# A hybrid transformer block on one core: modulation vectors as column-grouped TensorE products, and the convolution norm moved behind its last taps

## The chip, the cores and the metric

The kernel runs on one core of a Trainium2 chip. The metric is the device time of one execution in microseconds. Three runs of the kernel before gave 1427.99, 1431.49 and 1431.73 us, a median of 1431.49. The engines are named as in the profile: PE is TensorE (PEld its weight loads), DVE is VectorE, ACT is ScalarE, POOL is GpSimd, and SP is the engine that issues every DMA of this kernel. Each engine works through its own queue in a fixed order.

## The reference

One block of a network over 512 tokens of width 1024, with 256 context tokens, all in 32-bit floats:

```
mod_x = split((silu(c) @ w_ada + b_ada), 6)          # six vectors of 1024; the same of c_ctx for the context
h  = rmsnorm(x, g_norm1) * (1 + mod_x[1]) + mod_x[0] # hc the same of ctx with mod_c
u_rw, u_cv, u_ml, u_gate = split(h @ w_in)           # the RWKV and mLSTM parts also of hc
ya = rwkv mixer (8 heads, both directions)           # a state recurrence over context and tokens
yc = mlstm mixer (4 heads, both directions)
yb = silu(layernorm(depthwise_conv(a * sigmoid(g)), cv_lnw, cv_lnb))   # 31 taps, 512 channels
x  = x + mod_x[2] * ((ga*(ya@p_a) + gb*(yb@p_b) + gc*(yc@p_c)) @ w_out) # ga, gb, gc = sigmoid(u_gate)
h  = rmsnorm(x, g_norm2) * (1 + mod_x[4]) + mod_x[3]
x  = x + mod_x[5] * (square(relu(h @ w_mlp1)) @ w_mlp2)
out = rmsnorm(x, g_final)
```

So vectors 0 and 1 are needed at once, and 2 to 5 only after the three branches.

## The kernel before, in words

Large matrix products are split: each operand is a rounded part (hi) and a rest (lo), and a product is three products, hi by hi, hi by lo and lo by hi. A half block of weights (128x512) is loaded by SP into a ring of three raw buffers (tag "raw", L149), ACT makes hi (L152) and POOL makes lo (L153). `dense` (L262) multiplies one block of 128 output columns with all tokens in 24 products. Small products in plain 32-bit floats stand in the trace as two instructions each.

The stages, in the order in which they are emitted:

- Prologue (L170 to L231). The tokens are normalized, the first two modulation vectors are made, and the modulated tokens are laid down transposed. The weights `wada` for vectors 0 and 1 are 8 loads of 1 MB into six buffers. For each of four groups of 512 columns, 8 products (L215) with a stationary operand of two columns (the silu of `c` and of `c_ctx`) are summed in two rows of PSUM, copied (L217), transposed in four pieces (L220) and applied.
- Convolution and operand stage (L276 to L473). Channel tiles 0 and 1 of the convolution are gated and go through their 31 taps on DVE (L291). Then, for each of four pairs of RWKV heads, `operands` (L338 to L394) makes what the recurrence reads, twice per pair: loads BK and rd from other tiles (L348 to L353), small products `plora` (L358), exponentials on ACT, two scans on DVE, products on POOL (L379 to L386) and DVE (L389, L393), and stores to DRAM. `values` (L434 to L442) follows for all pairs.
- mLSTM stage (L477 to L514): `front` and `back` of each of four heads. The taps of channel tiles 2 and 3 (L495) are emitted after `back(0)`; then the pool `CZ` that they use closes (L498), and the RWKV pool `rwa` opens in memory on the same side. Its first loads (L946) and the Gram products and inverses of the first pair (`ctx(0)`, `lat(0)`) are emitted there, before the heads that are left. Six gate blocks follow.
- RWKV stage (L517 to L690). For each of four pairs a chain of 12 steps with three phases each (L1113, L1119, L1128: a product on PE, an eviction on ACT, the new state on DVE at L1129). `weave` spreads over it the preparation of the next pair, the last pair's output, and products of `dense_`: the 18 other gate blocks (L531), then the projections of the convolution and the mLSTM (L610). In the last pair (j = 3) it also spreads `conv_norm` (L552 to L593), which loads the four convolution tiles, normalizes over channels and activates them, and `modulations` (L630 to L653), which makes vectors 2, 3 and 4: for each of six groups of 512 columns, 8 loads (L623) and 8 accumulations on DVE (L625, L627), then small products that sum over the partitions (L640, L651).
- Merge and MLP (`merge`, L1239 on). What is left of the modulations is emitted first (`for _ in mods: pass`), then the projection of the RWKV branch (L701), the output projection (L1281), the second norm, and the MLP (L1350, L1281). The last vector is made in the same way inside the MLP's loop by `last_modulation`, after blocks 8 and 16, and read from DRAM at the end.

A planner fixes the order of each engine's queue ahead of the run, from estimated durations and with the order of emission as the priority (`schedule_with_timeline_sim=True`); the steps of the RWKV chain get a raise (`BOOST`), and what `weave` spreads is held behind the chain's last instruction on its engine (`paced`).

Of the kernel before, what the change touches and what calls it, by code (L numbers as in the profile page):

```python
# [7 lines left out]
F32 = mybir.dt.float32  # L8
# [52 lines left out]
def rsqrt(nc, S, x, n, name="rsq"):  # L61
    """1 / sqrt of the few columns x (overwritten): a first guess from the exponent, three Newton steps."""
# [14 lines left out]
def build(tc, wblk, wada, xin, cin, params, lora, consts, rowp, out, dbg=None):  # L77
# [42 lines left out]
    sc = K.tile([P, KT, 2], F32, name="sc")  # L120
# [13 lines left out]
    sp["m5", 0] = DR.tile([1, D], F32, name="sp_m5")  # L134
# [28 lines left out]
    # ------------------------------------------------------------------ norm, first modulation, hT  # L163
# [20 lines left out]
    V.tensor_tensor(sc.rearrange("p k c -> p (k c)"), tc_[:, :], C("cc", 0, 16), ALU.mult)  # L184
# [59 lines left out]
    # ------------------------------------------------------------------ input projections  # L244
# [23 lines left out]
    # ------------------------------------------------------------------ convolution branch  # L268
# [69 lines left out]
    def operands(j, h, kb, r):  # L338
        """What the products of head h of pair j read, for both directions, one on each half of the partitions."""
# [6 lines left out]
        # rows of the products with U and with V, in this order in the first half, swapped in the second  # L346
# [48 lines left out]

    t = shifted(12, True, "vj", 2)
# [5 lines left out]
    # keys and the normalized keys of every pair  # L402
# [42 lines left out]
    for j in range(4):  # L445
# [30 lines left out]
    # convolution and mLSTM branches  # L476
# [10 lines left out]
    eg.close()  # L487
    st = [None] * 4
    tiles = [(i, CZ.tile([P, 752], F32, name=f"cz{i}")[:, :], CZ.tile([P, NT], F32, name=f"cy{i}")[:, :]) for i in (2, 3)]
# [6 lines left out]
    for i, z, y in tiles:  # L496
        SY.dma_start(sp["yb", i][:, :], y)
# [1004 lines left out]
```

## Time and profile before

| what | value |
|---|---|
| median of three runs | 1431.49 us (1427.99 to 1431.73) |
| profiled execution: span from its first to its last instruction | 1429.6 us (the profile gives no other time for it) |
| granted TensorE clock, mean | 0.934 |
| PE, DVE, POOL, ACT busy | 1271.3, 903.0, 689.4, 496.4 us |
| bytes moved | 187.81 MB, mean 131 GB/s |
| 64 loads of 256 KB for vectors 2 to 5 (wad) | median 3.8 us from issue to landing |
| 296 loads of weight halves (raw) | median 2.8 us from issue to landing |
| DVE accumulations of vectors 2 to 5 (L627) | 56 instructions, 56.7 us |

Times are microseconds of one execution, from the span's start. Busy time is an average over stages with different limits, so the stages have to be read one by one. A PE instruction's duration in the profile is modelled and overlaps with the next one's; what one costs in a row of many is the distance between starts.

### The profile page before, as it was taken

The numbers are of one execution on the slowest core, as the hardware profiler recorded it, in microseconds if no ns is written. First come the engines' busy times: TensorE is split into PE (matmuls) and PEld (weight loads), VectorE is DVE, ScalarE is ACT, GpSimd is POOL, SyncE is SP. The second block draws the span as 40 slices with busy tenths as digits, with TensorE's granted clock in tenths as the row PEclk, the third lists the DMA queues.
The fourth block names the chain that finished last, engine by engine and source line by source line (L and its number), as shares of the span: only waits on it lengthen the run. The fifth ranks groups of instructions, "written<-read, shape, count | busy, mean of one in ns | idle before, by whom it ended". The sixth has DMA issues, their size and how long they took to land.

```text
span 1429.6 us, 21049 instructions
## 1 busy us (share of the span) xinstructions
PE 1271.3 (89%) x7620; PEld 985.8 (69%) x7620; DVE 903.0 (63%) x1518; ACT 496.4 (35%) x1024; POOL 689.4 (48%) x651
## 2 busy tenths in 40 slices
PE   6989986857698989789989998888999999999997
PEld 1578765635587877566757665566778888888886
DVE  2689888988736699379598895868657543300202
ACT  3422534423222222134244344532354344422322
POOL 0463499990854544233243344533455454444442
PEclk9999998887899998899699998999999999999999
DMA  9211466554162232433244134587544433343332
GB/s 363 67 60 58 119 182 205 171 182 147 39 185 72 93 107 67 128 101 100 72 135 117 45 97 156 185 258 231 205 153 146 134 111 96 111 144 99 125 96 88
DMA packets 113359, 187.81 MB, mean 131 GB/s; under 512 B 23124, under 2 KB 41812, under 8 KB 112232
## 3 DMA queue, kind: packets, MB, share of 16 engines
q1 hardware_dynamic: 113256, 186.47, 41.6%
q8 instruction: 60, 0.98, 0.3%
q14 instruction: 43, 0.35, 0.1%
HBM read 148.64 MB, written 29.40 MB: 125 GB/s over the span
## 4 chain that ended last, share of the span: by engine, by line
PE 58%; DVE 21%; DMA 7%; POOL 7%; issue 5%; ACT 2%; SPq 1%; DVEq 0%; POOLq 0%; ACTq 0%
PE pt L1281 15%; PE pd L1350 12%; PE dl L262 8%; PE dg L531 5%; POOL wlo L153 4%; PE pg L989 3%; DMA wad<-wada 3%; DVE N L1032 3%; PE pr L215 2%; DVE tmp L1030 2%; PE dc L262 2%; DVE cy L291 2%; POOL BK L386 1%; PE ch L1113 1%; DVE N L1025 1%
## 5 line engine op out<-in xcount | busy, mean ns | idle before, releaser
L153 POOL TENSOR_TENSOR wlo<-raw,whi 128x512 fp32r<-128x512 f32 x296 | 440.3, 1493 | 492.9 <-ACT whi L152 437.6
L152 ACT CAST whi<-raw 128x512 fp32r<-128x512 f32 x296 | 181.8, 618 | 358.1 <-PE pt L1281 113.8
L262 PE MATMUL dl<-hh,wlo 128*128 128x512 f32 (+1 forms) x368 | 153.6, 418 | 24.8 <-POOL wlo L153 24.7
L262 PE MATMUL dl<-hh,whi 128*128 128x512 f32 (+1 forms) x368 | 154.5, 420 | 0.7 <-DVE lf L716 0.7
L262 PE MATMUL dl<-hl,whi 128*128 128x512 f32 (+1 forms) x368 | 152.6, 415 | 0.0
L1376 DVE TENSOR_TENSOR x<-pt,modb 128x512 f32<-128x512 f32 x8 | 5.5, 689 | 154.7 <-PE pt L1281 154.7
L1350 PE MATMUL pd<-h2l,whi 128*128 128x512 f32 (+1 forms) x272 | 102.6, 379 | 0.7 <-POOL h2l L1333 0.7
L262 PEld LDWEIGHTS dl<-hh,wlo 128*128 128x128 f32 (+1 forms) x368 | 73.6, 200 | 42.1 <-POOL wlo L153 26.6
L1350 PE MATMUL pd<-h2h,wlo 128*128 128x512 f32 (+1 forms) x272 | 102.0, 377 | 0.0
L1350 PE MATMUL pd<-h2h,whi 128*128 128x512 f32 (+1 forms) x272 | 101.1, 378 | 0.2 <-ACT h2h L1330 0.2
L1281 PE MATMUL pt<-whi,h1l 128*128 128x512 f32 x256 | 99.6, 389 | 0.0
L1281 PE MATMUL pt<-whi,h1h 128*128 128x512 f32 x256 | 99.6, 389 | 0.0
L1281 PE MATMUL pt<-wlo,h1h 128*128 128x512 f32 x256 | 99.1, 389 | 0.0
L262 PEld LDWEIGHTS dl<-hh,whi 128*128 128x128 f32 (+1 forms) x368 | 73.8, 200 | 17.0 <-DVE lf L716 2.1
L262 PEld LDWEIGHTS dl<-hl,whi 128*128 128x128 f32 (+1 forms) x368 | 73.6, 200 | 15.0 <-issue 0.5
L1126 POOL TENSOR_TENSOR sps<-SV,PL 64x128 f32<-64x128 f32 x88 | 40.1, 455 | 79.0 <-DVE SV L1129 75.5
L1354 DVE TENSOR_TENSOR relu<-relu 128x512 f32<-128x512 f32 x32 | 39.5, 1238 | 56.0 <-ACT relu L1353 55.9
L627 DVE SCALAR_TENSOR_TENSOR accm<-wad,sc,accm 128x512 f32<-128x512 f32 x56 | 56.7, 1013 | 27.0 <-DMA wad<-wada 26.6
L531 PE MATMUL dg<-hh,whi 128*128 128x512 f32 x144 | 66.5, 462 | 0.0
L531 PE MATMUL dg<-hl,whi 128*128 128x512 f32 x144 | 66.4, 461 | 0.0
L531 PE MATMUL dg<-hh,wlo 128*128 128x512 f32 x144 | 65.6, 456 | 0.0
L989 PE MATMUL pg<-AL,BK 64*128 64x128 f32 (+1 forms) x384 | 59.1, 311 | 5.5 <-DVE AL L996 4.5
(388 smaller groups left out, 2942.0 us busy)
## 6 DMA issues: line engine op xcount, KB each, us to landing
raw<-wblk SPq DMA_DIRECT2D x296, 256.0 KB, 2.8
wad<-wada SPq DMA_DIRECT2D x64, 256.0 KB, 3.8
wada<-wada SPq DMA_DIRECT2D x8, 1024.0 KB, 17.5
sp_bk<-BK SPq DMA_DIRECT2D x8, 768.0 KB, 3.5
BK<-sp_bk SPq DMA_DIRECT2D x8, 768.0 KB, 4.5
sp_g<-gt SPq DMA_DIRECT2D x24, 256.0 KB, 2.1
sp_al<-al SPq DMA_DIRECT2D x8, 640.0 KB, 3.2
AL<-sp_al SPq DMA_DIRECT2D x16, 256.0 KB, 5.8
```

What stands on the lines that cost most here:

```text
L152: A.copy(hi[:, :], raw[:, :])
L153: G.tensor_tensor(lo[:, :], raw[:, :], hi[:, :], ALU.subtract)
L215: PE.matmul(pr[:, :], lhsT=sc[:, k, :], rhs=wa[q * 2 + k // 4][:, k % 4, :], start=(k == 0), stop=(k == KT - 1))
L262: PE.matmul(ps_[0:M, :], lhsT=w[:, ko:ko + M], rhs=x[seg][:, k, :], start=(n == 0), stop=(n == 3 * KT - 1))
L531: yield lambda w=w, x=x, k=k, ko=ko, n=n: PE.matmul(ps[:, :], lhsT=w[:, ko:ko + P], rhs=x[:, k, :], start=(n == 0), stop=(n == 3 * KT - 1))
L627: V.scalar_tensor_tensor(o, t[:, :], sc[:, k, 0:1], o, ALU.mult, ALU.add)
L989: PE.matmul(ps[:, i, :, :], lhsT=BK[dd, c, :, :], rhs=AL[d][dd, b0:b0 + w, :], start=True, stop=True)
L1032: V.tensor_tensor(N[:, s + 1:32, 0:s], N[:, s + 1:32, 0:s], tv, ALU.add)
L1126: last["Pool"] = G.tensor_tensor(sps[hf], SV[d][hf, c, :, :], PL[hf, c, :].unsqueeze(2).to_broadcast([64, 2, CH]), ALU.mult)
L1281: PE.matmul(pss[i][:, :], lhsT=x[:, k, ts_], rhs=w[:, :], start=(k == 0 and n == 0), stop=(k == nk - 1 and n == 2))
L1350: PE.matmul(ps[:, ts_], lhsT=w[:, ko:ko + P], rhs=x[:, k, ts_], start=(k == 0 and n == 0), stop=(k == 7 and n == 2))
L1354: V.tensor_tensor(t[:, :], t[:, :], t[:, :], ALU.mult)
```

## The change

All modulation products now use `partial`: block k of a group of 512 columns is multiplied with a stationary operand of 32 columns (the two silu columns of block k and what lies behind them) and written to the 32 PSUM partitions of column group k mod 4. Blocks 0 to 3 start a sum, blocks 4 to 7 end it. Four partial sums stand then in rows 0, 32, 64 and 96 (for `c_ctx` in the rows behind these). They are added by a product with `sel`, which has a one in those rows. In the prologue this takes the place of the sum in two rows and of the transposition. For vectors 2 to 5, `modulation(q)` is emitted in the operand stage, one group behind each call of `operands`. Its loads use the ring of raw weight buffers, its copies the buffer tagged "bo". Vectors 2 and 5 go to DRAM as rows and are read back as broadcasts; 3 and 4 are written to `b2` and `s2` at once. The DVE accumulations, `modulations` and `last_modulation` are gone, and `weave` for the last pair carries only the chain, the tail and `dense_`.

`conv_norm` is no longer a generator in the last pair. It is called behind the taps of tiles 2 and 3, on the tiles that are still there and on tiles 0 and 1 loaded again, in the pool `CZ`, and stores the four results. `projections` loads and splits them when it comes to them, and those of the mLSTM likewise only when it comes to these.

```diff
-    sc = K.tile([P, KT, 2], F32, name="sc")
+    scz = K.tile([P, 2 * KT + 30], F32, name="scz")
+    sel = K.tile([P, 2], F32, name="sel")
+    V.memset(scz[:, 2 * KT:], 0.0)
+    V.tensor_tensor(sel[:, :], ident[:, 0:2], ident[:, 32:34], ALU.add)
...
+    def partial(ps, k, w):
+        g = slice(32 * (k % 4), 32 * (k % 4) + 32)
+        PE.matmul(ps[g, :], lhsT=scz[:, 2 * k:2 * k + 32], rhs=w, start=(k < 4), stop=(k >= 4))
...
-        pr = PS0.tile([2, NT], F32, tag="pr", name="pr", bufs=2)
+        pr = PS0.tile([P, NT], F32, tag="pr", name="pr", bufs=2)
         for k in range(KT):
-            PE.matmul(pr[:, :], lhsT=sc[:, k, :], rhs=wa[q * 2 + k // 4][:, k % 4, :], start=(k == 0), stop=(k == KT - 1))
-        row = S0.tile([2, NT], F32, tag="row", name="row", bufs=2)
+            partial(pr, k, wa[q * 2 + k // 4][:, k % 4, :])
+        row = S0.tile([P, NT], F32, tag="row", name="row", bufs=2)
         A.copy(row[:, :], pr[:, :])
...
-            PE.transpose(pt[:, i, :], row[:, i * P:(i + 1) * P], ident[0:2, 0:2])
+            PE.matmul(pt[:, i, :], lhsT=row[:, i * P:(i + 1) * P], rhs=sel[:, :], start=True, stop=True)
...
+    def modulation(q):
+        ps = PSD.tile([P, NT], F32, tag="d", name="pq", bufs=ND)
+        for k in range(KT):
+            w = W0.tile([P, 512], F32, tag="raw", name="wad", bufs=NRAW)
+            SY.dma_start(w[:, :], wada[8 + q * 2 + k // 4][:, k % 4 * 512:k % 4 * 512 + 512])
+            partial(ps, k, w[:, :])
+        row = S1.tile([P, NT], F32, tag="bo", name="row")
+        A.copy(row[:, :], ps[:, :])
+        if 2 <= q < 6:
+            pc = PS1.tile([P, 4], F32, tag="n", name="pc", bufs=2)
+            for i in range(4):
+                PE.matmul(pc[:, i:i + 1], lhsT=row[:, i * P:(i + 1) * P], rhs=sel[:, 0:1], start=True, stop=True)
...
+        else:
+            m, x = q // 6, slice(q % 2 * 512, q % 2 * 512 + 512)
+            pc = PS1.tile([P, NT], F32, tag="n", name="pc", bufs=2)
+            PE.matmul(pc[0:1, :], lhsT=sel[:, 0:1], rhs=row[:, :], start=True, stop=True)
+            br = S1.tile([P, NT], F32, tag="bo", name="br")
+            SY.dma_start(br[0:1, :], rowp[m:m + 1, x])
+            V.tensor_tensor(br[0:1, :], pc[0:1, :], br[0:1, :], ALU.add)
+            SY.dma_start(sp["m", 2 + 3 * m][:, x], br[0:1, :])
...
             operands(j, h, kbs[j], rj)
+            modulation(2 * j + h)
...
+    def conv_norm(late):
+        ys = []
+        for i in range(2):
+            y = CZ.tile([P, NT], F32, name=f"cy{i}")
+            SY.dma_start(y[:, :], sp["yb", i][:, :])
+            ys.append(y[:, :])
+        ys += late
...
+        for i in range(1, 4):
+            G.tensor_tensor(total[:, :], total[:, :] if i > 1 else ys[0], ys[i], ALU.add)
...
+            V.scalar_tensor_tensor(ys[i], th, 1.0, ys[i], ALU.add, ALU.mult)
+            SY.dma_start(sp["yb", i][:, :], ys[i])
...
     taps(tiles)
-    for i, z, y in tiles:
-        SY.dma_start(sp["yb", i][:, :], y)
+    conv_norm([y for _, _, y in tiles])
     ec.close()
...
-        ys = {1: acc["yb"], 2: [operand(sp["yc", i]) for i in range(4)]}
         for b in (1, 2):
+            ys = [operand(sp[("yb", "yc")[b - 1], i]) for i in range(4)]
...
-    mods = modulations()
-    norm = conv_norm()
-    rw.weave(3, dense_, norm, mods)
+    acc["mod2b"] = acc["pool"].tile([P, D], F32, name="mod2b")
+    SY.dma_start(acc["mod2b"][:, :], sp["m", 2][:, :].partition_broadcast(P))
+    rw.weave(3, dense_)
...
-    for _ in mods:
-        pass
...
-        if fs[0] in (8, 16):
-            last_modulation(5 + fs[0] // 8, S, PS)
```

## Rows read from the trace of the kernel before

**Rows 1.** The page, the chain that ended last: shares of the span by engine.

```profile
PE 58%; DVE 21%; DMA 7%; POOL 7%; issue 5%; ACT 2%; SPq 1%; DVEq 0%; POOLq 0%; ACTq 0%
```

**Rows 2.** Stages: length, busy PE, PEld, DVE, ACT, POOL, clock, DMA share, GB/s.

```profile
180.00:322.00 142.00, 100.64 (x436) 76.32 (x434) 120.13 (x82) 55.01 (x91) 136.69 (x116) 0.86 0.62 186
...
407.00:494.00 87.00, 83.17 (x495) 71.50 (x494) 46.31 (x143) 21.39 (x40) 44.71 (x50) 0.96 0.40 119
494.00:596.00 102.00, 82.78 (x580) 68.92 (x578) 83.59 (x212) 23.45 (x44) 38.49 (x41) 0.88 0.29 94
...
863.00:942.00 79.00, 64.93 (x493) 43.73 (x492) 54.52 (x98) 37.10 (x98) 39.90 (x41) 0.91 0.58 186
942.00:1020.00 78.00, 70.00 (x326) 55.90 (x326) 61.00 (x93) 20.77 (x35) 27.66 (x19) 0.96 0.78 251
```

**Rows 3.** Timeline of the prologue: start, us, engine, line, operation, tiles, count.

```profile
13.07 6.44 PE L215 MATMUL pr<-wada,sc 128*2 128x512 f32 x8 [13.07 <-DVE rs0t L71]
...
40.78 7.03 PE L215 MATMUL pr<-wada,sc 128*2 128x512 f32 x16
...
54.79 0.79 PE L262 MATMUL dl<-hh,whi 128*128 128x512 f32 x1
```

**Rows 4.** The stage table's columns for two short stretches of the prologue.

```profile
28.00:30.00 2.00, 2.00 (x6) 0.42 (x5) 0.00 (x0) 1.15 (x2) 0.00 (x0) 1.00 1.07 422
...
34.00:36.00 2.00, 2.00 (x6) 0.43 (x5) 2.00 (x3) 1.34 (x3) 2.00 (x2) 1.00 0.41 135
```

**Rows 5.** Timeline of PE near 938 us, output products in two column halves.

```profile
938.38 0.22 PE L1095 MATMUL py<-LR,UU 128*64 128x64 f32 x1
938.43 0.22 PE L1094 MATMUL py<-AL,SV 128*64 128x64 f32 x1
938.44 0.22 PE L1095 MATMUL py<-LR,UU 128*64 128x64 f32 x1
```

**Rows 6.** Waits of SP (100 to 322 us), PE and DMA issues (180 to 322).

```profile
SPq L149 <- POOL wlo L153: 73.3, 24, 19.5
...
PE tp L434 <- DVE bo L441: 21.6, 3, 13.6
...
raw<-wblk SPq DMA_DIRECT2D x23, 256.0 KB, 4.2
```

**Rows 7.** Timelines of SP, DVE and PE: first RWKV load, last inverse, first step.

```profile
407.34 0.43 SPq L946 DMA_DIRECT2D BK<-sp_bk  x1
...
555.34 8.53 DVE L1055 STREAM_TRANSPOSE LT<-N 32x1024 f32<-32x1024 f32 x4
...
596.12 1.15 PE L1113 MATMUL ch<-SV,AL 128*64 128x64 f32 x6 [4.29 <-DMA SV<-sp_v]
```

**Rows 8.** Groups by line, 860 to 942 us: count, busy us, mean ns, idle before.

```profile
L627 DVE SCALAR_TENSOR_TENSOR accm<-wad,sc,accm 128x512 f32<-128x512 f32 x19 | 21.1, 1112 | 7.2 <-DMA wad<-wada 7.0
...
L569 DVE TENSOR_TENSOR macc<-macc,mean 128x512 f32<-128x512 f32 x4 | 3.6, 955 | 2.9 <-ACT mean L567 2.9
...
L590 DVE TENSOR_SCALAR macc<-macc,dv 128x512 f32<-128x512 f32 x4 | 2.3, 584 | 0.0
...
L573 POOL TENSOR_TENSOR ctot<-ctot,csq 128x512 f32<-128x512 f32 x3 | 4.3, 1430 | 0.9 <-ACT UV L1122 0.8
```

**Rows 9.** Timeline of PE: phases of the last pair's chain, its waits in brackets.

```profile
866.52 0.46 PE L1113 MATMUL ch<-SV,AL 128*64 128x64 f32 x8
...
867.80 0.46 PE L1119 MATMUL ch<-xc,LT 64*64 64x64 f32 x8
...
875.46 1.01 PE L1113 MATMUL ch<-SV,AL 128*64 128x64 f32 x8 [4.17 <-DVE SV L1129]
...
937.54 0.60 PE L1113 MATMUL ch<-SV,AL 128*64 128x64 f32 x5 [1.86 <-ACT UU L1132]
```

**Rows 10.** The chain of waits, a full stretch of PE; PE groups by line.

```profile
1020.45 41.72 PE pt L1281 x184
...
L663 PE MATMUL pmr<-accm,ones 128*1 128x512 f32 x4 | 2.0, 591 | 0.0
```

More of the change, by code (lines that the diff above doesn't have):

```diff
@@ L133, in build @@
         sp["z", i] = DR.tile([P, 752], F32, name=f"sp_z{i}")
-    sp["m5", 0] = DR.tile([1, D], F32, name="sp_m5")
+    for m in (2, 5):
+        sp["m", m] = DR.tile([1, D], F32, name=f"sp_m{m}")
     sp_rows = [DR.tile([4, T], F32, name=f"sp_rows{i}") for i in range(4)]
@@ L487, in build @@
     eg.close()
+    def conv_norm(late):
[5 more added lines that the diff above has]
+        ys += late
+        wide = lambda name: CZ.tile([P, 752], F32, tag="cz", name=name, bufs=2)[:, 0:NT]
+        total = CZ.tile([P, NT], F32, name="ctot")
+        for i in range(1, 4):
+            G.tensor_tensor(total[:, :], total[:, :] if i > 1 else ys[0], ys[i], ALU.add)
+        pl = PSD.tile([P, NT], F32, tag="d", name="cn", bufs=ND)
+        PE.matmul(pl[:, :], lhsT=ones[:, :], rhs=total[:, :], start=True, stop=True)
+        mean = wide("mean")
+        A.activation(mean, pl[:, :], AF.Copy, scale=1.0 / 512)
+        for i in range(4):
+            V.tensor_tensor(ys[i], ys[i], mean, ALU.subtract)
+            sq = total[:, :] if i == 0 else wide("csq")
+            A.activation(sq, ys[i], AF.Square)
+            if i:
+                G.tensor_tensor(total[:, :], total[:, :], sq, ALU.add)
+        pv = PSD.tile([P, 4], F32, tag="d", name="cv", bufs=ND)
+        for t in range(4):
+            PE.matmul(pv[:, t:t + 1], lhsT=total[:, t * P:(t + 1) * P], rhs=ones[:, 0:1], start=True, stop=True)
+        vs = CZ.tile([P, 4], F32, name="vs")
+        V.tensor_scalar(vs[:, :], pv[:, :], 1.0 / 512, 1e-5, ALU.mult, ALU.add)
+        r = rsqrt(nc, CZ, vs[:, :], 4)
+        cr = PSD.tile([P, NT], F32, tag="d", name="cr", bufs=ND)
+        for t in range(4):
+            PE.matmul(cr[:, t * P:(t + 1) * P], lhsT=r[:, t:t + 1].to_broadcast([P, P]), rhs=ident, start=True, stop=True)
+        for i in range(4):
+            V.tensor_tensor(ys[i], ys[i], cr[:, :], ALU.mult)
+            th = wide("cth")
+            A.activation(th, ys[i], AF.Tanh, scale=lwh[:, i:i + 1], bias=lbh[:, i:i + 1])
+            V.tensor_scalar(ys[i], ys[i], lwh[:, i:i + 1], lbh[:, i:i + 1], ALU.mult, ALU.add)
+            V.scalar_tensor_tensor(ys[i], th, 1.0, ys[i], ALU.add, ALU.mult)
+            SY.dma_start(sp["yb", i][:, :], ys[i])
     st = [None] * 4
-    tiles = [(i, CZ.tile([P, 752], F32, name=f"cz{i}")[:, :], CZ.tile([P, NT], F32, name=f"cy{i}")[:, :]) for i in (2, 3)]
+    tiles = [(i, CZ.tile([P, 752], F32, tag="cz", name="cz", bufs=2)[:, :], CZ.tile([P, NT], F32, name=f"cy{i}")[:, :]) for i in (2, 3)]
     for i, z, y in tiles:
@@ L690, in build @@
     ehl.close()
-    merge(tc, nc, whalf, split, CN, C, ident, ones, epsc, sp, sp_x2, s2, b2, xin, rowp, out, dump, acc, ep, epp, ya, mods, last_modulation)
+    merge(tc, nc, whalf, split, CN, C, ident, ones, epsc, sp, sp_x2, s2, b2, xin, rowp, out, dump, acc, ep, ya)
     es.close()
@@ L1153, in paced, with weave @@
             fn()
-    def weave(self, j, dense, norm=(), mods=()):
+    def weave(self, j, dense):
         n = 3 * NCH
@@ L1171, in weave @@
                 self.paced(last, step(prev))
-            if j == 3:
-                self.paced(last, step(norm))
-            for _ in range(PACE[p] if j < 3 else self.MODS):
+            for _ in range(PACE[p] if j < 3 else 0):
                 self.paced(last, step(nxt))
@@ L1189, in weave @@
                 self.paced(last, f, ("PE",))
-        self.run(chain, *((nxt,) if j < 3 else ()), prev, out)
+        self.run(chain, nxt, prev, out)
         if j < 3:
@@ L1239, in tail, with merge @@
         yield
-def merge(tc, nc, wload, split, CN, C, ident, ones, epsc, sp, sp_x2, s2, b2, xin, rowp, out, dump, acc, ep, epp, ya, mods, last_modulation):
+def merge(tc, nc, wload, split, CN, C, ident, ones, epsc, sp, sp_x2, s2, b2, xin, rowp, out, dump, acc, ep, ya):
     V, A, G, PE, SY = nc.vector, nc.scalar, nc.gpsimd, nc.tensor, nc.sync
@@ L1254, in merge @@
     yh, yl = zip(*ya)
-    for _ in mods:
-        pass
     for dp in range(4):
```

105 lines of the change are left out of this document (12 added, 93 removed).

## The prediction

> **What bounds the kernel now.** I read the chain of waits first, then a table of stages, then each stage that the diff touches. No engine bounds all of it: the chain is 58% PE, 21% DVE, 7% DMA and 7% POOL [rows 1]. The stage table shows why one edit can be worth much in one place and nothing in another [rows 2]. The prologue (0 to 55 us) is a chain of modulation products on PE. The operand stage (180 to 322) belongs to POOL, 136.69 of 142 us, and PE is busy for 100.64 only. 407 to 494 is PE's (83.17 of 87) with DVE half idle (46.31). 494 to 596 is shared. 863 to 942, the last RWKV pair, is nobody's: PE 64.93 of 79, DVE 54.52, a chain of short steps. 942 to 1020 is PE's with holes, and behind it PE runs without a gap.
>
> **Prologue.** A product of the old form (8 row blocks, 512 columns, each product two instructions) takes 7.03 us for 16, 0.44 each [rows 3]; the first 8, at 13.07, took 6.44, and the last group ends at 47.8, so four groups hold PE for over 30 us. Their weights do not take so long: the DMA runs at 422 GB/s up to 30 us and has fallen to 135 by 34 [rows 4], so the last weights lie there at about 34. The new products write 32 of the 128 columns of the array, and four may run side by side. That different column parts do run together, two instructions of a product and all, is in the trace: L1095 in one half starts at 938.38 and 938.44, and L1094 in the other half at 938.43 between them [rows 5]. With four abreast a group is 4 x 0.44 = 1.8 us, at the pace of the first eight (0.8 each) 3.2, which is less than the 2 MB of a group take to come (5 us at 422 GB/s). The loads set the end: 34 + 1.3 for what is left of the last group, then what now lies between the last product at 47.8 and the first projection at 54.79, 7 us: 42.3, or 12 us sooner. The row copy covers 128 partitions in place of 2, with the same 512 columns, so I leave its price; the transposition becomes 8 instructions in place of 4, a microsecond in the four groups. Bounds: minus 15 (the context's norm also moves into the waits for loads) to plus 2 (no concurrency, more transpositions). I take **-12**.
>
> The Trainium skill speaks against the full fourfold gain (TensorE: Matmul & The Clock Gate, Part 3, "What overlaps and what doesn't"): matmuls start and end strictly in program order. By it the second instruction of a product would hold back the next column group, and a group would take 9 x 0.44 = 4 us instead of 1.8. The trace does not agree for column halves, since the two starts of one product have another product's start between them [rows 5]; no row shows four groups. It stands below as a rival.
>
> **Operand stage.** Added: 8 groups of products, 64 loads of 256 KB, 8 row copies on ACT, 4 x 4 + 4 small products and a few DVE instructions of 4 columns or one row. On PE that is 128 x 0.44 / 4 = 14 us abreast, and some 7 for the sums over the four groups (32 and 8 instructions, the latter 0.44 each): 21 us; unpaired it would be 56 + 7 = 63. PE stands idle for 41 of the 142 us here, and POOL, which sets the end, gets nothing to do. So the products hide. What may not hide are the loads. They take turns in the ring of three raw buffers of the projections' weights, and SP, which issues all DMAs in order, already waits 73.3 us there for POOL to free one [rows 6]. Behind a waiting load stand the BK and rd loads that POOL's own work needs. Also 16.8 MB in 142 us are 118 GB/s more on 186 at 0.62 busy: about 1.0, so transfers will come later. And `row` and `br` share the one "bo" buffer with the values, whose products already keep PE waiting 21.6 us [rows 6]. Bounds: minus 3 (more work on PE keeps the granted clock, now 0.86, up) to plus 90 (each of 64 loads a third of the 4.2 us that a raw load takes to land [rows 6], none absorbed). I take **+8**, near the lower end, because the row nearest to it is PE's idle 41 us beside POOL's full ones, and the planner that orders the queues knows the ring.
>
> **Convolution norm behind its last taps.** 16 DVE instructions of 512 columns at 0.584 to 0.955 [rows 8] are at most 15 us, with the root 17; 6 sums on POOL at 1.43 are 8.6; ACT some 6, PE 3.5. DVE has 40 us free between 407 and 494, POOL 42. The length of it counts more than the work: sum, mean, squares, root, broadcast, activation, one after the other, about 24 us. The pool that it lives in closes behind it, and the first RWKV operand load, now at 407.34, waits for that memory. The inverses that these loads lead to end at 564, and the first step of the chain that reads them stands at 596 [rows 7]: 32 us of slack against 24. If the cover were gone all 24 would show. Late next would be the inverse's vector steps, which then fall among the last heads' of the mLSTM, where DVE is busy for 83.59 of 102 us. Bounds 0 to +24; **+4**.
>
> **Last RWKV pair.** Out of DVE's queue go 19 accumulations (21.1 us) with their 7 us of waiting for loads, and the norm; out of PE's some 5 us of products. The effect is on the chain's steps. A step without company takes 1.28 (866.52 to 867.80); the 30 steps from 866.52 to 937.54 average 2.37, and one of them waits 4.17 us for a DVE that itself waits for a load [rows 9]. Bounds: -5 (PE's products alone) to -33 (all 30 at 1.28). PE's remaining work is 64.93 - 5.4 = 59.5 of the 79 us, so the floor without a better clock is -19.5. I take **-16**: near that floor, since DVE drops from 54.5 to about 15 us. The yb operands now come by load and split instead; they wait for no one else.
>
> **Projections behind it.** From 942 to 1020 there remain 154 products of the convolution and mLSTM and 96 of the RWKV branch; at 41.72 / 184 = 0.227 [rows 10] that is 56.8, with the last pair's tail 59. New is a wait: the mLSTM operands are now made only when the buffers of the convolution's are free, so their first split (one ACT cast, one DVE difference, some 2.5 us with the hand-overs) falls between two products; behind it stand all later products in PE's queue. Add 2 for what remains of holes: 64 in place of 78, **-14**. Bounds -19 (no hole) to -6 (holes stay, only the 40 products of the modulations go). SP no longer waits on these loads ahead of the gate loads.
>
> **MLP.** The two late modulations leave 16 loads, 16 DVE instructions nobody waits for, and 4 products of 0.44 in a PE that has no gap [rows 10]: **-2**.
>
> Sum: -12 + 8 + 4 - 16 - 14 - 2 = -32. On the profiled span of 1429.6 that is 1397.6. The median of the runs is 1431.5, 1.9 us more for what lies around the span, so **1399**.
>
> **Rivals.** (a) Column groups in strict order: the prologue is still set by the loads, 1.3 us worse, and the operand stage has 17 us more PE work, most of it in the idle time: +4, 1404. For it: no row with four groups. Against: rows 5. (b) The last pair is not bound by DVE: the steps wait on ACT and semaphores, only the PE items go (-5) and holes in the projections stay (-9): 1415. For it: the wait of 1.86 us for ACT at 937.54. (c) No concurrency at all, the change not doing what it says: prologue 0, operand stage +25: 1428. Against: rows 5. (d) The operand stage gives it back, about +37: 1428 to 1433, no change. For it: DMA near 1.0 and the 73.3 us of SP. (e) **Slower**: the ring of raw buffers. A load for a modulation waits for a buffer that a weight half holds until POOL reaches it; SP stands still, and the BK loads behind it starve POOL. Price: up to 1.4 us for each of 64 loads; it decides from 40 / 64 = 0.63 us each, where the 44 us of gains less 4 for the norm are eaten. At 0.85 it is 54 us: 1446. Against: POOL's two operand buffers, and that weights and modulations are both wanted by the same queue order.
>
> **Chances.** Forecast 0.45, (a) 0.13, (b) 0.14, (c) 0.07, (d) 0.09, (e) 0.12. A measurement tells from no change what is over 0.3%, 4.3 us: faster is below 1427.2. Faster: forecast, (a), (b), and not quite half of (c) and (d), 0.79; the same: the rest of these, 0.09; slower 0.12. The range: below, the prologue's -15, the steps at -25 and an operand stage that costs nothing give 1377; above it takes in (b), (c) and (d) to 1433 and leaves out (e). The forecast's own range is 1384 to 1414.
>
> **What would show it.** Right: the first projection near 42 us; four starts of the new products within 0.1 us, 16 of them in under 4; POOL still full in the operand stage, and that stage not over 10 us longer; the RWKV chain's first step at about 15 us after its inverses or more; steps of the last pair near 1.8; no hole over 3 us in the projections. Wrong: SP waiting for raw buffers much beyond 73 us with POOL idle beside it; new products 0.44 us apart; the first chain step directly behind the last inverse; the last pair still near 2.4 a step.

## The result, and the profile after

The changed kernel takes 1516.17 us (median of four runs, 1513.22 to 1519.96) against 1430.82 of the kernel before: a ratio of 1.060, 95% interval 1.057 to 1.063. Forecast were 1399 us. The profiled spans are 1518.1 and 1429.6 us, the mean granted clocks 0.921 and 0.934. The runs of some kernels below fall into a faster and a slower group (one run each of e2 and e4 and five of the ten of e6 are in the slower one), and ratios with their intervals are taken from the faster group, while the times given are medians of all runs.

Both executions cut at the same events, in us; the last columns are runs told of below, whose traced executions took 1438.1 us (e1, median 1432.05) and 1404.0 us (e7, median 1414.80). The last g2 copy is ACT's last copy of the RWKV output gate (L471 in the kernel before), with which the operand stage ends; the chain's last step is its last product at L1113:

| stretch | before | after | after - before | e1 | e7 |
|---|---|---|---|---|---|
| start to first projection | 54.8 | 46.6 | -8.2 | 47.4 | 46.9 |
| to the last g2 copy (operand stage) | 289.4 | 406.0 | +116.6 | 299.6 | 298.3 |
| to the first step of the RWKV chain | 251.9 | 244.6 | -7.3 | 257.9 | 253.9 |
| to its last step | 342.0 | 325.6 | -16.4 | 334.7 | 322.1 |
| to the first output projection | 79.0 | 83.4 | +4.4 | 83.3 | 67.6 |
| to the end | 412.5 | 411.9 | -0.6 | 413.4 | 413.4 |

One stretch explains the sign. The stage table of the changed kernel (columns as in [rows 2]), the operand stage in two parts, then the mLSTM's, the last pair and the projections:

```profile
180.00:322.00 142.00, 96.86 (x263) 35.91 (x262) 96.20 (x75) 43.06 (x64) 84.13 (x81) 0.82 0.75 212
322.00:453.00 131.00, 104.66 (x467) 76.33 (x468) 85.71 (x112) 36.21 (x61) 60.21 (x49) 0.86 0.35 109
...
597.00:697.00 100.00, 80.56 (x592) 66.99 (x590) 75.27 (x203) 23.66 (x44) 37.94 (x41) 0.90 0.30 96
967.00:1026.00 59.00, 55.01 (x469) 36.53 (x468) 17.49 (x47) 32.42 (x91) 27.56 (x35) 0.94 0.53 169
1026.00:1106.00 80.00, 66.45 (x296) 52.49 (x295) 42.21 (x63) 20.23 (x34) 24.98 (x20) 0.89 0.48 151
```

From 180 to 322 PE executed 263 instructions where it had executed 436 [rows 2], and POOL fell from 136.69 [rows 2] to 84.13 us. What is missing from both, the dense blocks of the values and gates and the weight halves that feed them, stands in the next 131 us. The heads' own operands are not late: the last BK store is issued at 324.4, before at 319.1. The DMA issues between 140 and 325 us say it most plainly (count, size, median us to landing where it is given). After:

```profile
wad<-wada SPq DMA_DIRECT2D x61, 256.0 KB
...
raw<-wblk SPq DMA_DIRECT2D x7, 256.0 KB
```

Before:

```profile
raw<-wblk SPq DMA_DIRECT2D x30, 256.0 KB, 4.1
```

Thirty weight halves became seven; 61 modulation loads went through the three buffers in their place. The waits of SP (100 to 322 us) and of PE (180 to 322) show how a turn passes: SP waits for a buffer until the product has read it, PE waits for the load.

```profile
SPq L414 <- PE pq L174: 40.3, 31, 8.2
SPq L414 <- POOL wlo L160: 13.3, 5, 8.0
...
SPq L156 <- POOL wlo L160: 9.2, 3, 4.1
```

```profile
PE pq L174 <- DMA wad<-wada: 37.1, 19, 5.3
```

In [rows 6] SP stood 73.3 us for POOL on behalf of the weights; now it is 9.2 up to 322 us, since most of the weight halves come later. POOL no longer sets the pace, it waits for others, here 33.3 us for the exponentials of one kind:

```profile
POOL PL L394 <- ACT E L380: 33.3, 4, 10.8
POOL al L392 <- DMA BK<-kb: 10.3, 3, 6.5
```

The products themselves, in the timeline of PE (start, us, then what; idle before in brackets):

```profile
196.22 1.04 PE L174 MATMUL pq<-wad,scz 128*32 128x512 f32 x2
...
202.46 1.04 PE L174 MATMUL pq<-wad,scz 128*32 128x512 f32 x2 [1.06 <-DMA wad<-wada]
207.40 2.63 PE L174 MATMUL pq<-wad,scz 128*32 128x512 f32 x4 [3.89 <-DMA wad<-wada]
```

They come singly (x2 is one product, x4 two), since one load at a time has landed. In the prologue, where 1 MB of weights lies there, the same form runs abreast:

```profile
20.55 1.07 PE L174 MATMUL pr<-wada,scz 128*32 128x512 f32 x8
...
33.49 1.94 PE L174 MATMUL pr<-wada,scz 128*32 128x512 f32 x8 [3.41 <-DMA wada<-wada]
38.82 1.26 PE L215 MATMUL pl<-cst,ct 128*128 128x128 f32 x4 [3.40 <-DVE ct L211]
40.01 1.94 PE L174 MATMUL pr<-wada,scz 128*32 128x512 f32 x8
...
46.64 0.80 PE L275 MATMUL dl<-hh,whi 128*128 128x512 f32 x1 [1.06 <-ACT xnT L216]
...
47.66 0.63 PE L275 MATMUL dl<-hh,wlo 128*128 128x512 f32 x1
48.09 0.63 PE L275 MATMUL dl<-hh,whi 128*128 128x512 f32 x1
...
52.68 0.39 PE L275 MATMUL dl<-hh,wlo 128*128 128x512 f32 x1
```

Eight instructions, four products in four column groups, take 1.07 us where [rows 3] has 0.44 an instruction. By the strict order of the Trainium skill (TensorE: Matmul & The Clock Gate, Part 3, "What overlaps and what doesn't") I had worked out 4 us for a group of eight products. This trace does not show that price: such a group is two of these rows, 2.1 us.

### The profile page after: what moved, and what is told of

Read it like the earlier page. It is cut to its first block, busy times and chain, and to the rows that moved or that the text cites. A ratio compares the mean times of both kernels' runs of the same rounds, so it can differ in the third digit from the quotient of the medians.

```text
span 1518.1 us, 21259 instructions
## 1 busy us (share of the span) xinstructions
PE 1329.6 (88%) x7764; PEld 991.3 (65%) x7764; DVE 821.4 (54%) x1460; ACT 503.4 (33%) x1032; POOL 648.7 (43%) x651
## 5 line engine op out<-in xcount | busy, mean ns | idle before, releaser
L160 POOL TENSOR_TENSOR wlo<-raw,whi 128x512 fp32r<-128x512 f32 x296 | 423.6, 1436 | 529.4 <-ACT whi L159 490.3
L174 PE MATMUL pq<-wad,scz 128*32 128x512 f32 x128 | 68.3, 740 | 44.8 <-DMA wad<-wada 44.7
L1334 DVE TENSOR_TENSOR relu<-relu 128x512 f32<-128x512 f32 x32 | 43.5, 1361 | 84.8 <-ACT relu L1333 84.8
L174 PEld LDWEIGHTS pq<-wad,scz 128*32 128x32 f32 x128 | 9.3, 119 | 87.6 <-DMA wad<-wada 79.4
```

The source lines that it names most:

```text
L160: G.tensor_tensor(lo[:, :], raw[:, :], hi[:, :], ALU.subtract)
L174: PE.matmul(ps[g, :], lhsT=scz[:, 2 * k:2 * k + 32], rhs=w, start=(k < 4), stop=(k >= 4))
L1334: V.tensor_tensor(t[:, :], t[:, :], t[:, :], ALU.mult)
```

## The experiments

e1 to e4 asked where the operand stage's time goes. In all 18 runs the planner orders the queues anew, so some microseconds of each difference are order alone.

**e1_no_mod**: no modulation groups, vectors 2 to 5 constant.

```diff
             operands(j, h, kbs[j], rj)
-            modulation(2 * j + h)
```

Expected: 

> The changed kernel without the eight modulation groups of the operand stage: their 64 loads, 64 products, row copies and sums are left out and vectors 2 to 5 are constants. Prologue, convolution norm, last pair and projections stay as changed. Theory 1 (the operand stage loses its 114 us to the modulations alone) and rivals 2 (PE work of the products), 3 (DMA bandwidth) and 5 (the shared raw ring): the stretch from the first dense product to the last g2 copy falls from 406 us back to about 292, total 1516 - 114 = 1402, 1395 to 1410. Rival 4 (the moved convolution norm or the later operands cost much of it, hidden behind the long stage): 1420 or more.

1432.05 us, ratio 1.003 (1.001 to 1.006). The modulations cost 84 us net, 1.3 us for each of 64 loads, less than the 116.6 of the table. And the rest of the change, forecast to gain 44 us, gains nothing. Two questions, then.

**e2_one_load** and **e3_narrow**: eight products on one load; eight loads for products of 64 columns.

```diff
-            w = W0.tile(...); SY.dma_start(w[:, :], wada[...])
+            if k == 0: w = W0.tile(...); SY.dma_start(w[:, :], wada[8 + q * 2][:, 0:512])   # e2
-            partial(ps, k, w[:, :])
+            partial(ps[:, 0:64], k, w[:, 0:64])                                             # e3
```

Expected of e2: 

> Each group loads one tile of 256 KB and all eight of its products read it (seven eighths of the loads are left out, the values of vectors 2 to 5 are wrong); the same 64 products in the same places. Theory 1 (loads arrive singly, so products run one at a time and the queue of PE waits between them): four run abreast, PE time of the products 68 -> about 20 us, waits nearly gone, total 1405 to 1430. Rival 2 (PE work of the products in this place is too much): still above 1470. Rivals 3 and 5 also expect 1405 to 1430.

Expected of e3: 

> All 64 loads through the shared ring as in the changed kernel, but each product reads only 64 of its 512 columns (the rest of vectors 2 to 5 is left out). Products cost some 0.06 us an instruction in place of 0.43. Theory 1: of 68 + 45 us the 68 fall to about 10, but the waits between single loads stay or grow as the products no longer fill them, 1450 to 1490. Rival 2 (the PE work): 1400 to 1430. Rivals 3 and 5 (loads and their ring): no gain, 1500 to 1520.

1439.15 (ratio 1.008, 1.005 to 1.011) and 1507.64 (1.055, 1.053 to 1.058). All the products with an eighth of the loads cost 7 us more than none; all the loads with an eighth of the columns save 9 of 1516. So my first theory, products that run one at a time, falls: it is the loads. It had expected e3 at 1450 to 1490. (In e3, and in e5 below, POOL also fills the rest of each row with zeros, eight instructions more.)

**e4_own_ring** and **e5_small_loads**: four own buffers and four products behind four loads; and e3 with 32 KB a load.

```diff
-            w = W0.tile([P, 512], F32, tag="raw", name="wad", bufs=NRAW)
+            w = SO.tile(..., tag=("z0", "z1", "cy0", "cy1")[k % 4], name="wad")[:, 0:512]   # e4
+            if k % 4 == 3: products of the last four, in reverse order
-            SY.dma_start(w[:, :], wada[...][:, k % 4 * 512:k % 4 * 512 + 512])
+            SY.dma_start(w[:, 0:64], wada[...][:, k % 4 * 512:k % 4 * 512 + 64])            # e5
```

Expected of e4: 

> The loads of the modulations leave the shared raw ring for four buffers of their own (memory that the first two convolution tiles no longer need); four loads are issued together and the four products run in reverse order, so that all four have their data when the first starts. Nothing is left out. Theory 1: 16 bursts of about 1.1 us with one wait each; products 18 us on PE, stage 20 to 45 us longer than before the change in place of 114, total 1420 to 1450. Rival 3 (DMA bandwidth): as many bytes in the same place, above 1490. Rival 2: PE work is a quarter, so also 1420 to 1450. Rival 5 (only the shared ring matters): 1410 to 1430.

Expected of e5: 

> As e3_narrow (products over 64 columns, the rest of vectors 2 to 5 left out), and the 64 loads through the shared raw ring bring only these 64 columns, 32 KB in place of 256. Same number of loads, same ring slots, same order in SP's queue, an eighth of the bytes. Theory A (what costs is that each load takes a turn in the weights' ring and in SP's queue, and the weights behind it wait): little changes, 1485 to 1510. Theory B (the bytes: DMA share 0.8 to 0.95 in this stage): near e2_one_load, 1435 to 1455.

1469.44 (1.029, 1.025 to 1.032) and 1478.76 (1.036, 1.031 to 1.040). The DMA issues of the same 140 to 325 us, e5, e4 and the loads of e3:

```profile
raw<-wblk SPq DMA_DIRECT2D x20, 256.0 KB, 3.4
...
wad<-wada SPq DMA_DIRECT2D x61, 32.0 KB, 1.8
```

```profile
wad<-wada SPq DMA_DIRECT2D x60, 256.0 KB, 5.2
...
raw<-wblk SPq DMA_DIRECT2D x16, 256.0 KB, 3.5
```

```profile
wad<-wada SPq DMA_DIRECT2D x61, 256.0 KB, 4.8
```

From e2 to e3 56 more loads cost 68.5 us; with an eighth of the bytes 28.9 of them go, and 39.6 stay. Neither rival holds alone: the price of a load is its turn in a buffer, and the turn is shorter where the load lands sooner (1.8 us in e5, 4.8 in e3). e4 keeps all the bytes and SP's one queue; its own buffers, and four products behind four loads, take 47 us off the changed kernel's time. The number of weight halves that get through by 325 goes with the time: 30 before, 28 in e1, 25 in e2, 20 in e5, 16 in e4, 14 in e3, 7 in the changed kernel (1427, 1432, 1439, 1479, 1469, 1508, 1516 us). Only e4 stands out of line, with its own buffers and fewer single waits of PE. Those waits are a second way in which a load costs: what stands behind such a product in PE's queue waits with it. From 100 to 322 us, in e3, e5 and e4:

```profile
PE pq L174 <- DMA wad<-wada: 69.8, 38, 7.5
```

```profile
PE pq L174 <- DMA wad<-wada: 29.0, 22, 4.2
```

```profile
PE pq L174 <- DMA wad<-wada: 22.9, 10, 9.0
```

No run separates these waits from the turns that the weight halves lose; both come with the loads.

**e8_mod_behind_taps** and **e13_ring15**: the groups behind the taps of tiles 2 and 3, in four or fifteen buffers of their own; mLSTM operands as in e7.

```diff
     taps(tiles)
+    for q in range(8):
+        modulation(q)          # w = CZ.tile([P, 512], F32, tag="wad", bufs=4)   e13: bufs=15
     conv_norm([y for _, _, y in tiles])
```

Expected of e8: 

> All of the change, nothing left out, but the modulations emitted behind the taps of tiles 2 and 3, with four buffers of their own and four products after each four loads, and the mLSTM operands made early as in e7. PE was busy there for only 19 to 26 of 40 us (340 to 380) and the DMA share is 0.2. Theory A (the loss in the operand stage is the weights waiting behind these loads): that stage returns to about 300 us, the products cost at most 15 here, total 1420 to 1440. Theory B (the bytes cost wherever they are): 1455 to 1470.

Expected of e13: 

> e8_mod_behind_taps with one number changed: fifteen buffers of its own in place of four for the modulation loads. Nothing left out. In e8 the products and loads took turns from 430 to 545 us with every other engine nearly still (PE busy 16 of 40, DMA share 0.4, clock 0.5). Theory A, turns: a load's price is its place in a short ring (issue, landing, product, free again); with fifteen the loads run ahead beside the taps at a higher DMA share, the first RWKV load comes 15 to 40 us after e7's 451 instead of 111, total 1430 to 1455. Theory B, bytes: 16.8 MB cost as much as in e8, 1505 to 1525.

1520.48 (1.064, 1.059 to 1.068) and 1460.87 (1.024, 1.020 to 1.028). e8 refutes what I expected and shows the mechanism bare, since nothing else was left to run there. 80 us of its stage table, and what PE and SP wait for from 420 to 550:

```profile
460.00:540.00 80.00, 31.77 (x129) 9.79 (x122) 9.03 (x42) 4.03 (x7) 0.00 (x0) 0.53 0.40 135
```

```profile
PE pq L174 <- DMA wad<-wada: 51.5, 13, 5.6
```

```profile
SPq L546 <- DMA wad<-wada: 46.1, 14, 4.0
SPq L546 <- PE pq L174: 29.9, 15, 2.5
```

The turns of four loads start 6.9 to 8.3 us apart, 7.7 on average: 1 MB in 7.7 us is the 135 GB/s of the row, at a DMA share of 0.40. Buffers set that rate, not the DMA. With fifteen, the DMA moves twice as much in the same place (other loads included):

```profile
420.00:475.00 55.00, 45.40 (x279) 26.35 (x281) 29.65 (x134) 8.97 (x16) 12.27 (x18) 0.86 0.82 271
```

and the kernel takes 60 us less. The first fifteen loads were issued from 317 to 329 already, but then the ring stood still until their first products, which the planner had put behind dense blocks (e13, PE and then SP):

```profile
422.94 1.93 PE L174 MATMUL pq<-wad,scz 128*32 128x512 f32 x16
```

```profile
424.02 3.18 SPq L546 DMA_DIRECT2D wad<-wada  x7
```

**e14_six_groups**, **e16_six_ahead**, **e17_six_spread** follow from it: e13 with vector 5 back in the MLP on DVE; its six groups ahead of the first mLSTM head; and two by two.

```diff
-    for q in range(8): modulation(q)        # e13, behind the taps
+    for q in range(6): modulation(q)        # e14: there; e16: ahead of st[0] = front(0)
```

Expected of e14: 

> e13_ring15 with vector 5 back on DVE inside the MLP as in the kernel before, so six groups and 48 loads behind the taps. Nothing left out. Theory A: a quarter of e13's extra time goes, and the MLP pays at most 2 us: 5 to 10 us below e13, 1420 to 1445, which may be below both kernels. Theory B: 25 to 30 us below e13.

Expected of e16: 

> e14_six_groups with the six groups emitted ahead of the mLSTM's first head instead of behind the taps. Nothing left out. In e13 no modulation load was issued before 424, since SP stood behind weight loads that wait for POOL (28.7 us in one piece), although DMA was busy 0.19 and PE 24 of 40 us from 340 to 380. If the loads come first, they and the products fall into that stretch: 1420 to 1435, which may be below the kernel before. Rival (what is ahead in PE's queue then delays the mLSTM's projections by as much): 1440 to 1455.

Expected of e17: 

> As e16_six_ahead, but two groups ahead of the first head, two ahead of the second and two behind it. Nothing left out. Same theory, 1420 to 1435, with less of the products in one piece; if the order in SP's queue behind POOL's waits is what counts, between e16 and e14.

1453.31 (1.016, 1.010 to 1.022), 1435.24 (1.005, 1.003 to 1.008) and 1440.27 (1.009, 1.006 to 1.012). e14 lies 8 us below e13, as theory A had it, though above its range of 1420 to 1445, and e17 lies between e16 and e14. In e16 the groups fall into the stretch that DVE bounds with the taps, and the DMA there is at 0.75:

```profile
320.00:385.00 65.00, 37.06 (x161) 13.71 (x162) 60.86 (x98) 13.49 (x19) 4.59 (x5) 0.61 0.75 257
```

(What e16's expectation says of e13, no load before 424, was misread: fifteen had been issued, none released.) e16 is 81 us below the changed kernel, and still not below the kernel before.

**e9_mod_last**, e4's buffers with the groups behind the values:

```diff
         operands(j, h, kbs[j], rj)
-            modulation(2 * j + h)
...
+    for q in range(8): modulation(q)        # ahead of e2.close()
```

Expected: 

> All of the change, nothing left out; the modulations of e4_own_ring (own four buffers, four products behind four loads) emitted behind the values and g2, at the end of the operand stage instead of between its heads; mLSTM operands early as in e7. Theory A (the loss is that weight halves and their dense blocks wait behind modulation loads): the dense blocks come first again, first bo near 270, and only what the modulations themselves take is left; a turn of four loads took 5 to 6 us in e8, 16 of them 80 to 95 us, of which the operand stage's waits and the taps of tiles 2 and 3 cover a part: 1440 to 1475. Theory B (the bytes cost wherever they are): 1470 or more.

1492.93 (1.045, 1.041 to 1.050): the dense blocks come first again (bo, the first tile of the values, at 271.4 us, in the changed kernel at 391.2), the first RWKV load 83 us later than in e7 (534.0 to 451.1). The same loads in four buffers cost 37 us between the heads (e4 against e1), 78 here and 106 behind the taps (e9 and e8 against e7): behind the taps, where nothing else was left to run, most of the turns shows. My range was too low.

**e7_no_mod_yc** took the second question, the projections:

```diff
+        yy = {b: [operand(sp[("yb", "yc")[b - 1], i]) for i in range(4)] for b in (1, 2)}
         for b in (1, 2):
-            ys = [operand(sp[("yb", "yc")[b - 1], i]) for i in range(4)]
+            ys = yy[b]
```

Expected: 

> e1_no_mod (modulations of vectors 2 to 5 left out), with the mLSTM operands loaded and split together with the convolution's at the start of the projections, as in the kernel before. Theory (the projections lose their predicted 14 us to the 9.4 us hole in which the fourth mLSTM operand waits behind the last pair's tail in ACT's queue, and to the clock that falls in it): from last chain phase to the next projection 83 -> 68 to 74 us, total 1418 to 1424. Rival (the wait moves to the RWKV operands, which need the same eight buffers): 1428 to 1434.

1414.80 (0.992, 0.989 to 0.995), 17 below e1. In the changed kernel a product of the projections waits for ACT, and ACT for POOL:

```profile
1058.91 1.22 PE L647 MATMUL dp<-yh,whi 128*128 128x512 f32 x2 [9.41 <-ACT yh L167]
```

```profile
1057.72 0.62 ACT L167 CAST yh<-y 128x512 fp32r<-128x512 f32 x1 [10.34 <-POOL y L1217]
1058.24 1.66 ACT L167 CAST yh<-yld 128x512 fp32r<-128x512 f32 x3
```

The casts of the mLSTM operands stand in ACT's queue behind that of the RWKV tail. The stretch in e1 and in e7:

```profile
941.00:1023.00 82.00, 68.23 (x310) 53.73 (x309) 42.27 (x63) 21.07 (x38) 25.21 (x20) 0.90 0.49 152
```

```profile
922.00:989.00 67.00, 66.17 (x314) 52.39 (x313) 41.22 (x62) 20.71 (x38) 25.82 (x20) 1.00 0.57 182
```

PE busy changes by 2 us, the stretch by 15: idle went, and with it the lower clock. The order of the operands decides this stretch in every run without DVE accumulations of vectors 2 to 4: it took 82.8 to 83.6 us from the chain's last step to the first output projection in e1 to e5, and 66.8 to 67.7 in e7, e8, e9, e13, e14, e16 and e17, which make them together.

**e6_prologue_only** (the kernel before with `partial` and `sel` in the prologue only):

```diff
-            PE.matmul(pr[:, :], lhsT=sc[:, k, :], rhs=wa[q * 2 + k // 4][:, k % 4, :], start=(k == 0), stop=(k == KT - 1))
+            partial(pr, k, wa[q * 2 + k // 4][:, k % 4, :])
```

Expected: 

> The kernel before with the new prologue alone (column groups and sums by sel there; vectors 2 to 5 on DVE in the last pair as before; nothing left out). The first projection should start near 47 as in the changed kernel, 8 us sooner than before. If the gain lasts to the end: 1418 to 1423, ratio 0.992 to 0.996. Rival (it is eaten by what binds next, since in e1_no_mod the last store of the operand stage was 5 us sooner but the last g2 copy 3 us later): 1426 to 1432.

Median 1446.08 us, ratio 1.003 (0.998 to 1.008): no gain shows. Its ten runs go with the granted clock: 1425.0 us at 0.938, 1431.3 at 0.933, 1439.7 at 0.928, and six from 1445.6 to 1450.0 at 0.918 to 0.926. The only trace is of the run of 1445.6 us at 0.919, so it tells of that execution and not of the ratio. It has its first chain step at 588.5, 7.6 before that of the kernel before, and loses this again in the chain of the first pairs. There it has 40 us at a clock of 0.70 with PE busy nearly all the time; the second row is the kernel before, at the same distance from the chain's start:

```profile
760.00:800.00 40.00, 38.48 (x371) 28.67 (x368) 19.60 (x26) 11.99 (x29) 10.21 (x13) 0.70 0.28 80
```

```profile
752.00:792.00 40.00, 39.55 (x526) 29.79 (x522) 30.42 (x53) 17.59 (x48) 15.08 (x20) 1.00 0.35 100
```

From the chain's first step to the last pair's last 30 steps the four runs shown here execute the same 2493 or 2494 PE instructions. They are e11 (told of next; up to there its kernel emits what e6's does), the kernel before, e1 and e6, and the clock stands in the third column from the end:

```profile
592.03:855.03 263.00, 245.81 (x2493) 178.11 (x2493) 210.40 (x406) 103.15 (x290) 93.19 (x127) 0.95 0.35 105
```

```profile
596.12:866.52 270.40, 252.87 (x2494) 182.26 (x2494) 207.70 (x406) 103.72 (x290) 93.22 (x127) 0.91 0.35 102
```

```profile
604.86:886.83 281.97, 261.46 (x2494) 189.07 (x2494) 210.38 (x406) 103.51 (x290) 93.00 (x128) 0.87 0.33 98
```

```profile
588.52:874.61 286.09, 268.05 (x2494) 193.95 (x2494) 208.93 (x406) 103.31 (x290) 93.06 (x127) 0.86 0.33 97
```

The stretch gets longer as the granted clock falls, 23 us between e11's trace and e6's, and that is more than the prologue gains.

**e10_dve_late**, **e11_prologue_dve_late**, **e12_conv_moved**, **e15_sums_later**: vectors 2 to 4 on DVE as before, but behind the last pair.

```diff
-    MODS = 1
+    MODS = 0                # e10; e11: and the new prologue; e12: and the norm moved
...
-                for i in range(4):
-                    PE.matmul(pmc[...], lhsT=o[...], rhs=ones[:, 0:1], ...)
+                late.append((q, o))      # e15, on e12: multiplied behind the output projection
```

Expected of e10: 

> The kernel before with one constant changed: the DVE accumulations of vectors 2 to 4 are no longer spread over the last RWKV pair but all emitted behind it, beside the projections, where DVE was busy for 61 of 78 us with them partly in, and beside the output projection. Nothing left out. The prediction's step for the last pair says that its steps fall from 2.37 to about 1.8 us because these accumulations leave: -14 to -18 there. Theory (53 us of DVE work hide beside a full PE): 1410 to 1420. Rival (vector 2 is needed by the output projection and 3 and 4 by the MLP's input, so the loads and DVE come too late): 1428 to 1445.

Expected of e11: 

> e10_dve_late with the new prologue. Nothing left out. If the prologue's 8 us last to the end: 8 us below e10, 1402 to 1412. If they are eaten behind the prologue: as e10.

Expected of e12: 

> e11 with the convolution norm moved behind its last taps as in the changed kernel, and the operands of convolution and mLSTM loaded together at the start of the projections. So it is the changed kernel, but with vectors 2 to 5 on DVE behind the last pair. Nothing left out. The prediction's +4 for the move: 2 to 6 us above e11 less what the norm cost in the last pair. Rival: in e7 the first step of the chain stood 11 us later than the prologue's gain would have it (599.1, against 588.5 in e6), so 8 to 12 us above e11, unless the last pair gets shorter without the norm.

Expected of e15: 

> e12_conv_moved with the 16 small products that sum vectors 3 and 4 taken out of the stretch behind the last pair and emitted behind the output projection, each of the four sums in its own buffer. Nothing left out. In e12 PE waited 32.6 us in four of them for the DVE accumulations, with all the projections queued behind. Theory (a product in PE's queue that waits for loads holds up everything behind it, which is also how single modulation products cost in the operand stage): these 30 us go, 1435 to 1445. Rival (the accumulations themselves come too late for the second norm): 1455 to 1470.

1460.46 (1.022, 1.017 to 1.027), 1476.17 (1.034, 1.029 to 1.038), 1470.14 (1.028, 1.023 to 1.033) and 1442.47 (1.013, 1.007 to 1.018). e10 and e11 lie 40 and 64 us above what their theories expected, and e12 with them (6 below e11, near what was expected of the move), for a reason that is a relative of the operand stage's. PE of e10, 930 to 1110 us:

```profile
PE pmc L640 <- DVE accm L627: 34.4, 4, 13.0
```

Four small sums, each at the head of PE's queue, wait for accumulations that wait for loads in three buffers, and all projections stand behind them. e15 moves only these sums and gets 28 us back, as expected. The stages give the last pair's terms: 30 steps take 71.0 us before, 61.9 without the accumulations (e10), 51.2 without the norm too (e12; 62.4 in e11; the 48.5 in e18's expectation left phases out). And the norm's move puts the first chain step from 592.0 (e11) to 603.2 (e12). Why e11 is 16 us above e10 stays open: its trace is of its fastest run, 1457.3 us, and the others took 1474.7 to 1478.1.

**e18_norm_and_prologue**: the prologue and the norm's move, the accumulations where they were.

```diff
-    rw.weave(3, dense_, norm, mods)
+    rw.weave(3, dense_, iter(()), mods)
```

Expected: 

> The kernel before with the new prologue and the convolution norm moved as in the changed kernel; vectors 2 to 5 stay on DVE where the kernel before has them, and the operands of convolution and mLSTM are loaded together. Nothing left out. In e12 against e11 the move put the first chain step 11 us later (603.2 against 592.0) and took 14 us out of the last pair's 30 steps (62.4 to 48.5). If these cancel and the prologue's 8 us stay: 1418 to 1426, below both kernels. The prediction's terms (+4 for the move, and a share of the -16 for the last pair): 1412 to 1422. Rival: with the accumulations still in the last pair its steps stay near 2.2 us and the 11 us show: 1430 to 1440.

1432.49 (1.003, 0.999 to 1.006): the first chain step is at 603.9, 15 us later than in e6 (588.5), which has the norm where it was; the 30 steps take 59.8 us, 11 less than in e6 or the kernel before. The move costs 11 to 15 at one place and gives 11 back at the other; of the prologue's gain nothing is left. None of the versions that compute everything beats the kernel before.

## Why the prediction was wrong

**Operand stage, +8 forecast, 84 net (e1): the step that failed.** The prediction had the right bound, "each of 64 loads a third of the 4.2 us that a raw load takes to land", +90, and then took +8 "because the row nearest to it is PE's idle 41 us beside POOL's full ones". That row prices products, and products were never dear (7 us in e2). The term was loads, and their row was the other one: SP's 73.3 us at the ring [rows 6], which are of 222 us and not of the stage's 142, meant that weights already stood in line for the ring's turns. The sign that I had named for this, SP waiting much beyond 73 us, hardly shows: from 100 to 322 us SP now waits 84 us for raw buffers in all. What changed is for whom it waits, the modulations' products and loads in place of POOL, and POOL is idle for 58 of the 142 us.

Measured is 1.3 us a load, against 1.4 at the bound and 0.85 in rival (e). That rival had the mechanism but the wrong victim: not the BK loads (last store 5 us later) but the weight halves starve, and with them the dense blocks that had filled PE beside POOL. So the idle 41 us covered nothing (PE is idle for 45 of the same 142 us now): an engine's idle time covers work only if its input comes by a way that is free. That it is the loads is shown by e1, e2 and e3, that both the bytes and the ring have a part in it by e5 and e4; how much is the weights' lost turns and how much PE's waits for single loads is not. The 32 us between 84 and the 116.6 of the table are stretches in which e1 is slower too: 10 in the stage itself, and 13 up to the chain and 9 in the pairs against the changed kernel (the 9 at a clock of 0.87 in e1's first three pairs against 0.90).

**Projections, -14 forecast, +4 measured.** The steps (154 and 96 products, 59 us with the tail) hold: e7 gets 83.3 down to 67.6. Mis-sized was the new wait, 2.5 us for one split. It is 9.4, because I asked what stands behind the split in PE's queue and not what stands ahead of it in ACT's, where the RWKV tail's cast waits 10.3 us for POOL. Beside these 6.9 us more there are 3.8 in which PE waits for ACT in the tail, and PE is busy for 66.45 us where I had 59, at a clock of 0.89 for 0.96 [rows 2]: together that is about the difference of 18.

**Convolution norm, +4 forecast.** Its effect on the first chain step is 11 us (e11 to e12) or 15 (e6 to e18), within the bounds of 0 to 24: three to four times the term. In the changed kernel it did not show: the stretch to the chain is even 7 us shorter, though the slack behind the inverses fell from 32 us to 15.

**Last pair, -16 forecast, -19 measured** (30 steps in 52.1 for 71.0, 1.74 us a step). Right, and by the step named; e10 and e12 split it into 9 for the accumulations and 11 for the norm. Three phases without company:

```profile
982.49 0.46 PE L1105 MATMUL ch<-xc,LT 64*64 64x64 f32 x8
983.76 0.46 PE L1114 MATMUL ch<-UV,BKt 128*64 128x64 f32 x8
985.05 0.46 PE L1099 MATMUL ch<-SV,AL 128*64 128x64 f32 x8
```

**Prologue, -12 forecast, -8.2 measured.** Four abreast is right, rivals (a) and (c) fall. Missing: the planner put the context's transpositions, which wait 3.4 us for DVE, ahead of the last four products (eight instructions), so these start at 40.0, and wait for no load then. The first 13 projections then run at half clock, 0.43 apart, before they go on at full clock at 52.68. **MLP, -2**: nothing, 411.9 for 412.5.

The gains also did not add up: 7 in the prologue and 18.5 in the last pair stand in e1, and its time is that of the kernel before. By the table the operand stage takes 10 of them, the stretch to the chain 6 (into which the norm's move falls), the first three pairs 11 and the projections 4. The 11 of the pairs go with the clock, 0.87 for 0.91 over the same instructions (e1 and the kernel before, above); why it is lower there stays open. The lower end of the range, 1377, is mis-added as well: its three terms take 20 off 1399, which is 1379.

## What to carry to other kernels

Before hiding loads behind an engine's idle time, count turns: buffers, the time from issue through landing and use to free again, and who else takes turns. A ring whose issuer already waits has none to give, and the work that pays is the one that shares the ring, not the one that was added. Ask of each wait what stands ahead of it in its own queue, and of each in-order engine what a late operand at its head holds up.

## What was not expected of the hardware

A load's rate was set by buffers long before the DMA was full: 135 GB/s at a share of 0.40 with four buffers of 256 KB, 271 at 0.82 with fifteen, other loads included (e8, e13). And the granted clock differs between executions of one kernel, with its time: e6 from 0.938 at 1425.0 us to 0.919 at 1450.0. So a gain of 8 us in one stage can be outweighed in another: in e6's trace by 40 us at 0.70, 24 of them at 1.2 GHz, in a stretch in which PE was busy for 38.48 us.
